# A four-byte store per partition behind the sin table, with a memset that waits for it, in an interleaved-RoPE kernel

## The chip, the core and the metric

The kernel runs on one core of one Trainium2 chip. The metric is the device time in microseconds (us); lower is better. The profile is taken from one execution; its span (315.8 us before) is a little shorter than the device time (317.56 us), and all times inside the profile count from the start of that span. DVE is the vector engine, ACT the scalar engine, POOL the GpSimd engine, SP the sync engine. A queue name such as ACTq is the sequencer of that engine, where DMAs are issued. A packet is one record of the trace for the DMA engines; a semaphore packet is the four-byte one that reports the end of a transfer on one engine, and a transfer has landed when all of them have arrived. The records don't name the engine: 16 packets of one kind at one time are read here as one on each of the 16.

## The reference

Rotary embedding on interleaved pairs. x has shape (8, 2048, 16, 64), float32; cos and sin have shape (2048, 32).

```python
out1 = x1 * cos - x2 * sin      # x1, x2: even and odd elements of the last axis
out2 = x1 * sin + x2 * cos
out  = np.stack([out1, out2], axis=-1).reshape(x.shape)
```

## The kernel before

Each of the 128 partitions holds 16 rows of each of the 8 batches. The GpSimd queue loads a batch and casts it from float32 to bfloat16 on the way (8.4 MB read, 4.2 MB written), DVE rotates it in place, and the GpSimd queue stores it and casts it back. There are five tiles, so five loads can be issued at once; loads 5, 6 and 7 each reuse a tile and wait for a store to land. The first two rows of batch 0 come through the SP and Activation queues, as do the tables.

```python
    def load(b, k0=0):
        if b not in tiles:
            tiles[b] = xpool.tile([P, K, HD], bf16, name="xt")
        nc.gpsimd.dma_start(out=tiles[b][:, k0:], in_=x_t[b, :, k0:])

    def store(b, k1=K):
        nc.gpsimd.dma_start(out=out_t[b, :, :k1], in_=tiles[b][:, :k1])
# ... rotate(): three tensor_tensor on DVE for four rows: q = x*s, x = x*c, x = x + swap(q) ...
    with tc.manual_schedule():
        # ... two head rows of batch 0, one on the SP and one on the Activation queue ...
        nc.sync.dma_start(out=cos_sb, in_=cos_t)
        nc.scalar.dma_start(out=sin_sb, in_=sin_t)
        load(0, HEAD)
        for b in range(1, NX):
            load(b)
        # ... ACT casts the head rows; DVE builds s_tab and c_tab from sin_sb and cos_sb ...
        for b in range(B):
            # ... rotate batch b, four rows at a time ...
            if b < B - 1:
                store(b)
            if b >= 1 and b - 1 + NX < B:
                load(b - 1 + NX)
        store(B - 1, K - TAIL)
        # ... the last four rows: cast on ACT once store 6 has landed, store on SP ...
```

## Time and profile before

| what | value | where it is read |
|---|---|---|
| time, median of 3 | 317.56 us | runs |
| DVE busy | 221.8 us, 70% of the span | busy table |
| GpSimd DMA queue | 97.0% of the time of 16 DMA engines | queue table |
| first rotation on DVE | 25.05 us | timeline |
| DVE's waits for loads | 5.92 + 10.76 us | timeline |

The first fence has, from the page of the kernel before, the busy share of DVE and of the DMA engines in 40 equal slices (tenths; 9 is 90% or more), and the queue table (packets, MB, share of the 16 engines' span).

```profile
DVE  0009999999999999999999994799708996000000
DMA  9999999999999999999999999999999999999997
...
q0 software_dynamic: 2304, 98.04, 97.0%
q1 hardware_dynamic: 432, 2.88, 2.4%
q10 hardware_dynamic: 288, 0.79, 0.6%
```

The DMA row has no gap; DVE has gaps at the start, twice in the second half and at the end. The DMA engines are the bound. Queue q0 is GpSimd's, q1 SP's, q10 Activation's.

The next fence is the timeline of POOL before: start, length, engine, line, operation, output and input, and in brackets how long POOL stood idle before and what ended that. L56 is a load, L59 a store.

```profile
1.25 2.79 POOL L56 DMA_DIRECT2D xt<-in_x_dram  x5 [0.80 <-PEq L145]
54.07 0.54 POOL L59 DMA_DIRECT2D out_dram<-xt  x1 [50.03 <-DVE xt L80]
81.72 0.54 POOL L59 DMA_DIRECT2D out_dram<-xt  x1 [27.11 <-DVE xt L80]
121.98 0.53 POOL L56 DMA_DIRECT2D xt<-in_x_dram  x1 [39.72 <-DMA out_dram<-xt]
122.50 0.53 POOL L59 DMA_DIRECT2D out_dram<-xt  x1
141.30 0.53 POOL L56 DMA_DIRECT2D xt<-in_x_dram  x1 [18.27 <-DMA out_dram<-xt]
...
193.40 0.53 POOL L59 DMA_DIRECT2D out_dram<-xt  x1 [12.39 <-DVE xt L80]
227.21 0.53 POOL L59 DMA_DIRECT2D out_dram<-xt  x1 [33.27 <-DVE xt L80]
258.87 0.53 POOL L59 DMA_DIRECT2D out_dram<-xt  x1 [31.13 <-DVE xt L80]
```

Issue and transfer are two things. Store 0 was issued at 54.07 us, when DVE had finished batch 0. But the queue runs its transfers one after the other, and five loads were ahead of it. The times at which the transfers of this queue ended, from the semaphore packets in the packet records of the trace, are: loads 0 to 4 at 23.7, 43.0, 62.4, 81.7 and 102.0 us; store 0 at 121.3; store 1 at 140.6; load 5 at 160.0; store 2 at 179.3; and so on, one every 19.3 us (load 4 took 20.3). So store 0 had 48 us to spare before its turn came, and store 1 had 40.

Two lines of the timeline of DVE before show where it waited for loads in the second half:

```profile
25.05 1.22 DVE L74 TENSOR_TENSOR qt<-xt,s_tab 128x2048 bf16<-128x2048 bf16 x1
...
199.03 2.29 DVE L74 TENSOR_TENSOR qt<-xt,s_tab 128x4096 bf16<-128x4096 bf16 x1 [5.92 <-DMA xt<-in_x_dram]
...
237.67 2.29 DVE L74 TENSOR_TENSOR qt<-xt,s_tab 128x4096 bf16<-128x4096 bf16 x1 [10.76 <-DMA xt<-in_x_dram]
```

### The profile page before, as it was taken

The page shows a single profiled execution, that of the slowest core. Times are in us where ns is not written, and L with a number is a line of the kernel's source. Part 1 is how long each engine was busy: PE and PEld are TensorE (multiplying, and loading weights), DVE is VectorE, ACT ScalarE, POOL GpSimd, SP SyncE. Part 2 cuts the span into 40 slices and gives each one's busy share as a digit, 9 for nine tenths or more (in the row PEclk, how much of TensorE's full clock was granted, in tenths as well). Part 3 has the DMA queues.
Part 4 walks back from the last instruction along what each step waited for, and adds up shares of the span by engine and source line. Part 5 has one row for each costly group of instructions (what it writes and reads, how often), then busy time and mean ns, then how long its engine had stood idle before and what let it go on. Part 6 is the DMA issues. An engine that isn't in the chain of part 4 may idle for free.

```text
span 315.8 us, 198 instructions
## 1 busy us (share of the span) xinstructions
DVE 221.8 (70%) x102; ACT 6.9 (2%) x4; POOL 8.8 (3%) x20
## 2 busy tenths in 40 slices
DVE  0009999999999999999999994799708996000000
ACT  2100000000000000000000000000000000000400
POOL 3000000000000001010000100000000000000000
DMA  9999999999999999999999999999999999999997
GB/s 267 211 248 203 199 208 257 199 199 245 220 199 266 398 465 465 398 332 246 220 398 398 390 208 199 448 481 266 199 266 465 398 398 506 423 398 440 427 427 299
DMA packets 3025, 101.72 MB, mean 322 GB/s; under 512 B 336, under 2 KB 336, under 8 KB 848
## 3 DMA queue, kind: packets, MB, share of 16 engines
q0 software_dynamic: 2304, 98.04, 97.0%
q1 hardware_dynamic: 432, 2.88, 2.4%
q10 hardware_dynamic: 288, 0.79, 0.6%
q14 instruction: 1, 0.01, 0.0%
HBM read 67.63 MB, written 67.11 MB: 427 GB/s over the span
## 4 chain that ended last, share of the span: by engine, by line
another core or an unknown queue 91%; DMA 2%; ACTq 1%; ACT 1%; issue 0%
DMA st<-in_x_dram 2%; ACTq L145 1%; ACT xt L93 1%; ACT L93 0%; ACT xt L117 0%; ACTq L117 0%; ACTq L93 0%
## 5 line engine op out<-in xcount | busy, mean ns | idle before, releaser
L74 DVE TENSOR_TENSOR qt<-xt,s_tab 128x4096 bf16<-128x4096 bf16 (+1 forms) x33 | 73.5, 2228 | 17.7 <-DMA xt<-in_x_dram 16.7
L80 DVE TENSOR_TENSOR xt<-xt,qt 128x4096 bf16<-128x4096 bf16 (+1 forms) x33 | 73.5, 2228 | 1.1
L75 DVE TENSOR_TENSOR xt<-xt,c_tab 128x4096 bf16<-128x4096 bf16 (+1 forms) x33 | 73.5, 2228 | 1.1
L95 DVE CAST s_tab<-sin_sb 128x512 bf16<-128x512 f32 x1 | 0.5, 454 | 23.8 <-DMA sin_sb<-in_sin_dram 23.8
L59 POOL DMA_DIRECT2D out_dram<-xt x8 | 4.3, 533 | 153.9 <-DVE xt L80 153.9
L56 POOL DMA_DIRECT2D xt<-in_x_dram x8 | 4.4, 560 | 96.4 <-DMA out_dram<-xt 95.6
L117 ACT COPY xt<-xt 1x1 bf16<-1x1 bf16 x1 | 0.2, 194 | 286.8 <-DMA out_dram<-xt 286.8
L118 ACT CAST st<-xt 128x4096 f32<-128x4096 bf16 x1 | 3.6, 3598 | 0.0
L93 ACT CAST xt<-st 128x2048 bf16<-128x2048 f32 x1 | 1.9, 1897 | 0.0
L93 ACT ACT_TABLE_LOAD x1 | 1.3, 1283 | 5.7 <-DMA st<-in_x_dram 5.7
L97 DVE CAST c_tab<-cos_sb 128x1024 bf16<-128x1024 f32 x1 | 0.7, 684 | 0.0
L96 DVE TENSOR_SCALAR s_tab<-sin_sb 128x512 bf16<-128x512 f32 x1 | 0.4, 444 | 0.0
L134 POOL MEMSET const-float32-0.0<- 128x1 f32 x1 | 0.1, 99 | 0.2 <-issue 0.2
L134 POOL MEMSET const-bfloat16-1.0<- 128x1 bf16 x1 | 0.1, 102 | 0.0
L134 POOL MEMSET const-float32-1.0<- 128x1 f32 x1 | 0.1, 99 | 0.0
L134 POOL MEMSET const-uint8-127<- 128x1 uint8 x1 | 0.1, 99 | 0.0
## 6 DMA issues: line engine op xcount, KB each, us to landing
xt<-in_x_dram POOLq DMA_DIRECT2D x7, 4096.0 KB, 57.6
out_dram<-xt POOLq DMA_DIRECT2D x1, 6144.0 KB, 53.0
xt<-in_x_dram POOLq DMA_DIRECT2D x1, 3584.0 KB, 22.8
out_dram<-st SPq DMA_DIRECT2D x1, 2048.0 KB, 15.5
st<-in_x_dram ACTq DMA_DIRECT2D x1, 512.0 KB, 5.1
st<-in_x_dram SPq DMA_DIRECT2D x1, 512.0 KB, 4.9
sin_sb<-in_sin_dram ACTq DMA_DIRECT2D x1, 256.0 KB, 22.6
cos_sb<-in_cos_dram SPq DMA_DIRECT2D x1, 256.0 KB, 18.6
```

What stands on the lines that cost most here:

```text
L56: nc.gpsimd.dma_start(out=tiles[b][:, k0:], in_=x_t[b, :, k0:])
L59: nc.gpsimd.dma_start(out=out_t[b, :, :k1], in_=tiles[b][:, :k1])
L74: nc.vector.tensor_tensor(out=rows(qt[:, :nk]), in0=rows(xp), in1=tab(s_tab), op=mult)
L75: nc.vector.tensor_tensor(out=rows(xp), in0=rows(xp), in1=tab(c_tab), op=mult)
L80: nc.vector.tensor_tensor(out=x3, in0=x3, in1=q_swap, op=add)
L93: nc.scalar.copy(out=tiles[0][:, :HEAD], in_=head[:, :HEAD])
L95: nc.vector.tensor_copy(out=s2[:, :, 0], in_=sin_sb)
L96: nc.vector.tensor_scalar_mul(s2[:, :, 1], sin_sb, -1.0)
L97: nc.vector.tensor_copy(out=c_tab.rearrange("p k (i j) -> p (k i) j", j=2), in_=cos_sb.to_broadcast([P, K * D2, 2]),)
L118: nc.scalar.copy(out=tail, in_=tiles[B - 1][:, K - TAIL :])
L134: nc = _bacc.Bacc("TRN2", target_bir_lowering=False, num_devices=1)
L145: with _tile.TileContext(nc) as tc:
```

## The change

A tile of one float32 per partition is set to zero and written to the first element of each partition's first output row, over the Activation queue, behind the sin table. The real result of store 0 overwrites it later. After the tables have been built, the word is set to zero again. That second memset overwrites the source of the small store, so it must wait until the store has landed; and as it stands before the rotations in DVE's program, every rotation waits behind it.

```diff
         nc.scalar.dma_start(out=sin_sb, in_=sin_t)
+
+        word = consts.tile([P, 1], fp32)
+        nc.vector.memset(word, 0.0)
+        nc.scalar.dma_start(out=out_t[0, :, 0, :1], in_=word)
         load(0, HEAD)
 ...
             in_=cos_sb.to_broadcast([P, K * D2, 2]),
         )
+
+        nc.vector.memset(word, 0.0)
         for b in range(B):
```

## The prediction

> **What bounds the kernel now.** The 16 DMA engines. The queue table gives the GpSimd queue 97.0% of the engines' span, and the DMA row is full in every slice. DVE is busy 221.8 of 315.8 us. The chain of waits names almost nothing (91% "unknown queue"), so I went by the DMA packet records: the GpSimd queue runs its 16 transfers one after the other, about 19.3 us each (8 packets of 2.45 us per engine, load or store): five loads until about 102 us, store 0 to 122, store 1 to 141, load 5 to 160, store 2 to 179, load 6, store 3, load 7, stores 4 to 7; the tail store ends the span. There is no hole.
>
> **What the change does.** By the instruction order: a memset before the sin cast and one after the table build on DVE, a 128x1 store on the Activation queue behind sin. The second memset overwrites the word, so it waits for that store to land, and all rotations stand behind it on DVE.
> When does it land? In the packet records sin's 2 KB packets (8 per engine, 0.09 us each) went one per turn, each followed by a 2.1 us packet of load 0; sin landed 22.6 us after issue, with load 0. The Trainium skill, "DMA: Bandwidth & Descriptors", section "Queues, rings and completion order", says engines go round-robin between rows by packet; the trace agrees. The word store is 8 four-byte packets plus a semaphore packet per engine on the same ring, so it needs 8 to 9 turns beside load 1: 19.3 to 21.8 us after 23.8. I expect it at 43 to 46 us, and the first rotation at 44 to 46 us instead of 25.05.
>
> **How much is critical.** The shift (about 20 us) goes into slack: stores issue when DVE is done, but their turn in the full queue comes later. Before, batch ready against start of transfer: store 0 54 / 102, store 1 82 / 122, store 2 109 / 160, store 3 137 / 199, store 4 165 / 238. Shifted by 20: 74, 102, 129, 157, 185, all in time; the tightest (store 1) keeps about 20 us. Later loads wait for landings that don't move. DVE's two waits for loads (5.9 and 10.8 us, timeline) shrink to nothing and absorb 16.7 us, so DVE ends some 3 to 6 us later, about 270 us; store 7's turn is at 295. The tail waits for store 6 (295.6), unchanged.
> On the critical resource there remain the word's packets, 9 per engine. Four-byte semaphore packets took 0.01 to 0.04 us here, so 0.1 to 0.4 us, an estimate. The same page (section "Specifications") says transfers under 512 B cause a read-modify-write; no run here shows yet what a four-byte HBM write takes.
>
> **Predicted time: 317.9 us, 8 in 10 between 317.2 and 319.0. Faster by over 2%: 1%; within 2%: 96%; slower: 3%.**
>
> **What would show each step.** Waits: the second memset waits about 20 us for the word's store. Timeline: first rotation about 45 us; stores 0 and 1 issued 20 us later; loads 5, 6, 7 issued at unchanged 122, 141, 180 us. DVE's wait for loads near 0. DMA row still full.
>
> **What would make it wrong.** If small packets go several per turn, the shift is 3 to 5 us (same time). If the shift passes 40 us, store 1 misses its turn and the engines idle. If a four-byte HBM write blocks an engine for 1 us, 9 add 9 us (3%). If DVE activity slows packets (no sign: 2.43 to 2.45 us with DVE idle or busy).

## The result, and the profile after

After: 317.64 us median (317.43 to 318.0, 6 runs); before, in the same rounds: 317.54 us (317.42 to 317.64, 6 runs). The ratio is 1.0005 with a 95% interval of 0.9992 to 1.0018: the same. All runs of before lie within 0.22 us of each other. A ratio is the mean time of one kernel's fast runs over that of the other's of the same rounds, so it is not quite the ratio of the medians quoted.

The same rows of the page after:

```profile
DVE  0001049999999999999999999999999998000000
DMA  9999999999999999999999999999999999999997
...
q0 software_dynamic: 2304, 98.04, 97.0%
q1 hardware_dynamic: 432, 2.88, 2.4%
q10 hardware_dynamic: 432, 0.79, 0.7%
```

The DMA row is as full as before. Queue q10 has 144 packets more: 16 engines with 8 data packets and one semaphore packet each. DVE starts two slices later, and its gaps in the second half are gone.

The start of DVE, from its timeline after:

```profile
24.72 0.68 DVE L101 CAST c_tab<-cos_sb 128x1024 bf16<-128x1024 f32 x1
43.44 0.06 DVE L106 MEMSET word<- 128x1 f32 x1 [18.03 <-DMA out_dram<-word]
43.51 1.23 DVE L74 TENSOR_TENSOR qt<-xt,s_tab 128x2048 bf16<-128x2048 bf16 x1
```

The memset, 0.06 us long, waited 18.03 us for a store of 512 bytes, and the first rotation starts at 43.51 instead of 25.05 us: a shift of 18.46 us. The timeline of POOL after, to be read against the one of before:

```profile
1.25 2.79 POOL L56 DMA_DIRECT2D xt<-in_x_dram  x5 [0.81 <-PEq L151]
72.52 0.54 POOL L59 DMA_DIRECT2D out_dram<-xt  x1 [68.48 <-DVE xt L80]
100.17 0.54 POOL L59 DMA_DIRECT2D out_dram<-xt  x1 [27.11 <-DVE xt L80]
121.92 0.53 POOL L56 DMA_DIRECT2D xt<-in_x_dram  x1 [21.22 <-DMA out_dram<-xt]
128.08 0.53 POOL L59 DMA_DIRECT2D out_dram<-xt  x1 [5.62 <-DVE xt L80]
141.39 0.53 POOL L56 DMA_DIRECT2D xt<-in_x_dram  x1 [12.79 <-DMA out_dram<-xt]
...
260.65 0.53 POOL L59 DMA_DIRECT2D out_dram<-xt  x1 [20.40 <-DVE xt L80]
```

Stores 0 and 1 are issued 18.45 us later, load 5 at 121.92 against 121.98 us, load 6 at 141.39 against 141.30 us, and the last store only 1.78 us later. Of the shift of 18.46 us, 5.92 + 10.76 = 16.68 us went where DVE had waited for loads 6 and 7 before, and 18.46 - 16.68 = 1.78 us is left at the end. The transfers of the GpSimd queue ended at the same times as before, within 0.1 us.

Why did 512 bytes take 41.6 us from issue to landing? The packet records of the changed kernel answer it. This table, in an ordinary fence, is worked out from them: packets of one kind that started within 1 us of each other are one group (count, first and last start in us).

```
load 1, 32 KB written:  16: 23.10-23.68   16: 25.52-26.09   16: 27.93-28.51  ...  16: 40.01-40.58
Activation queue, 4 B:  32: 23.07-23.67   16: 25.51-26.09   16: 27.93-28.50  ...  16: 40.00-40.58   8: 42.50-43.00
```

Until about 23.1 us the word's packets stood behind sin's on their own queue. From then on each engine takes one four-byte packet, then one packet of load 1, which takes it 2.4 us, then the next four-byte packet: one turn each. (The first group has two on each engine, because load 0's semaphore packet also went between 23.08 and 23.65 us; eight of its 32 are sin's semaphore packets. Half of the engines were one packet ahead of the rest; their last packet went with the group at 40.00, that of the others at 42.50 us.) The words themselves took 0.009 to 0.022 us each.

### The profile page after: what moved, and what is told of

The parts are those of the page before. It is cut to its first block, busy times and chain, and to the rows that moved or that the text cites. A ratio compares the mean times of both kernels' runs of the same rounds, so it can differ in the third digit from the quotient of the medians.

```text
span 315.8 us, 204 instructions
## 1 busy us (share of the span) xinstructions
DVE 222.0 (70%) x104; ACT 6.9 (2%) x4; POOL 8.9 (3%) x20
## 4 chain that ended last, share of the span: by engine, by line
another core or an unknown queue 91%; DMA 2%; ACTq 1%; ACT 1%; issue 0%
DMA st<-in_x_dram 2%; ACTq L151 1%; ACT xt L97 1%; ACT L97 0%; ACT xt L123 0%; ACTq L123 0%; ACTq L97 0%
```

## The experiments

My theory has three parts. First, the delay is a matter of turns: a small store waits once per packet behind one large packet. Second, the shift of DVE costs nothing while each store is issued before its turn in the full queue. Third, the engines' time is what counts, and the word's packets take almost none of it. The rivals: the store takes long in itself (a fixed time, or slow four-byte writes); the shift costs something that the change gives back elsewhere; the shift never matters at all. All ten kernels gave correct results. The diffs are against the changed kernel.

### e1_no_wait: the store without the wait

```diff
-        nc.vector.memset(word, 0.0)      # the second one
```

> The word's store stays, the second memset goes, so that nothing on DVE waits for it. My theory (turns in the ring, shift swallowed by slack, packets nearly free): first rotation back at about 25 us, the store still lands at about 43 us, time within 0.2% of before. Rival (the wait itself costs something that the packets or something else gives back in the changed kernel): time differs from before by over 0.3%.

Measured: 317.44 us (317.40 to 317.48, 5 runs) against 317.44 us of before; ratio 1.0000, 0.9986 to 1.0014. One line of its DVE timeline:

```profile
25.21 1.22 DVE L74 TENSOR_TENSOR qt<-xt,s_tab 128x2048 bf16<-128x2048 bf16 x1
```

The first rotation was back at 25.21 us, and the store still took 41.5 us to land. The packets alone cost nothing that can be seen.

### e2_delay_only: the wait without the store

```diff
-        nc.vector.memset(word, 0.0)
-        nc.scalar.dma_start(out=out_t[0, :, 0, :1], in_=word)
 ...
-        nc.vector.memset(word, 0.0)
+        nc.vector.tensor_copy(out=word, in_=tiles[1][:, 0, :1])
```

> No word store at all; DVE instead copies one word of load 1 after the tables are built, so it waits for the landing of load 1. My theory: the wait ends at about 43.2 to 43.5 us as with the word's store (within 1 us), first rotation at 43.5 to 44.5 us, same issue times of all stores as in the changed kernel, time within 0.2% of before. Rival (the delay of DVE costs or gains time of itself): a difference over 0.3%.

Measured: 317.51 us (317.49 to 317.70, 5 runs) against 317.44 us; ratio 1.0003, 0.9991 to 1.0016. One line of its DVE timeline:

```profile
43.45 0.15 DVE L104 CAST word<-xt 128x1 f32<-128x1 bf16 x1 [18.07 <-DMA xt<-in_x_dram]
```

A wait for load 1 ends at the same moment as the wait for the word (43.45 against 43.44 us), and the stores are issued at 72.55 and 100.19 us as in the changed kernel. Together with e1_no_wait: neither half of the change costs or gains time, so nothing was being cancelled. It also fits the turns, by which the word lands with load 1.

### e3_two_words, e4_three_words, e5_four_words: how much slack there is

```diff
-        nc.scalar.dma_start(out=out_t[0, :, 0, :1], in_=word)
+        for c in range(2):               # 3 and 4 in the others
+            nc.scalar.dma_start(out=out_t[0, :, 0, c : c + 1], in_=word)
```

> Two word stores, one behind the other, and the memset waits for both. My theory: the second lands one load later, at about 62.6 us; first rotation at about 63 us (shift 37.7); store 0 ready at 92 against its turn at 102, store 1 at about 119.5 against its turn at 121.5: still just in time, time within 0.5% of before. Rival (no such slack; each us of shift beyond the first few costs): some 10 to 20 us slower.

> Three word stores: landing at about 82 us, shift 57. My theory: stores 0 and 1 miss their turns. Store 0 is ready at 111 with the queue empty since 102 (hole of about 9 to 10 us), store 1 at 139 with the queue empty since 130 (hole of about 9 us); together about 19 us, time about 336.5 us (333 to 340). The DMA row shows two dips near 102 and 130 us. Rival (the shift never matters, as it is off the path): about 317.7.

> Four word stores that DVE waits for: landing at about 102 us, shift 76.5. My theory: past the slack the time grows with the shift one to one: about 19 us more than with three word stores, about 356 us (351 to 361); the holes are each about 28.5 us after 102 us and about 9 us before store 1. Rival (growth of another slope, as the loads that come later fill the holes): under 345.

| stores of a word | memset waited, us | store 0 issued | store 1 issued | time, us | ratio to before (95%) |
|---|---|---|---|---|---|
| 1 (the change) | 18.0 | 72.52 | 100.17 | 317.64 | 1.0005 (0.9992 to 1.0018) |
| 2 | 37.5 | 92.06 | 119.70 | 317.71 | 1.0008 (0.9995 to 1.0022) |
| 3 | 56.7 | 111.26 | 138.91 | 336.77 | 1.0608 (1.0594 to 1.0623) |
| 4 | 76.1 | 130.41 | 158.05 | 356.58 | 1.1228 (1.1212 to 1.1243) |

Each further store adds 19.2 to 19.5 us of wait, the length of one load. With two, the timeline of POOL has stores 0 and 1 so:

```profile
92.06 0.54 POOL L59 DMA_DIRECT2D out_dram<-xt  x1 [88.02 <-DVE xt L80]
119.70 0.54 POOL L59 DMA_DIRECT2D out_dram<-xt  x1 [27.10 <-DVE xt L80]
```

Store 1 was issued 1.4 us before store 0's transfer ended (121.1 us), and the time did not move. This was the very edge: store 1's first packets started at 120.80 us, 1.1 us after the issue, and by then most of the engines had ended store 0 (they ended it between 120.2 and 121.1 us), so that they stood empty for 0.25 us on average. The slack thus ends about 1.1 us before the turn itself. With three, both stores came too late. The stages in which that shows, by windows of the profile (window, length, busy time of DVE, ACT and POOL with counts, clock, share of the DMA engines, GB/s), first with three words:

```profile
95.00:101.00 6.00, 5.93 (x3) 0.00 (x0) 0.00 (x0) 1.00 0.81 175
101.00:114.00 13.00, 12.80 (x7) 0.00 (x0) 0.54 (x1) 1.00 0.19 81
114.00:130.00 16.00, 15.76 (x8) 0.00 (x0) 0.00 (x0) 1.00 1.07 459
130.00:142.00 12.00, 11.83 (x6) 0.00 (x0) 1.07 (x2) 1.00 0.21 87
142.00:160.00 18.00, 17.73 (x9) 0.00 (x0) 0.00 (x0) 1.00 1.09 437
```

and the same windows of the changed kernel with its one word:

```profile
95.00:101.00 6.00, 5.90 (x4) 0.00 (x0) 0.54 (x1) 1.00 0.96 175
101.00:114.00 13.00, 12.80 (x7) 0.00 (x0) 0.00 (x0) 1.00 1.12 479
114.00:130.00 16.00, 15.80 (x7) 0.00 (x0) 1.06 (x2) 1.00 0.93 397
130.00:142.00 12.00, 11.79 (x7) 0.00 (x0) 0.53 (x1) 1.00 1.03 394
142.00:160.00 18.00, 17.76 (x8) 0.00 (x0) 0.53 (x1) 1.00 1.08 262
```

(A packet is counted in the window in which it starts, so shares can pass 1.) With three words the DMA engines are mostly empty around 101 to 114 and 130 to 142 us, before store 0 and before store 1; DVE is as busy in both kernels. By the packet records load 4 ended at 101.1, store 0 at 131.8 and store 1 at 159.5 us; less 19.3 us each for the transfers, the holes, in which the queue had nothing to move, are 11.4 and 8.4 us. From there on a transfer ended every 19 to 20 us again. With four words load 4 ended at 101.2, store 0 at 151.0 and store 1 at 178.6 us: holes of 30.5 and 8.3 us. The time rose by 19.3 us from before to three words (336.77 - 317.44) and by 39.0 us to four (356.58 - 317.60, of the other rounds), 19.7 us more for 19.15 us more of shift. With three words store 1 was issued 138.91 - 121.3 = 17.6 us after its turn had come in the kernel before, and its transfer ended 20.6 us after its issue in place of 19.3, as its first packets started only at 140.0 us, 1.1 us after the issue: together 18.9 of the 19.3 us that were lost. Both rivals, a cost per us of shift and no cost at all, are ruled out: the cost is zero up to the slack, and about one to one beyond, by the two kernels past it.

### e6_sixteen, e7_sixtyfour: packets per engine

```diff
-        nc.scalar.dma_start(out=out_t[0, :, 0, :1], in_=word)
+        nc.scalar.dma_start(out=out_t[0, :16, 0, :1], in_=word[:16])   # :64 in the other
```

> The word is written on 16 partitions alone: one data packet and one semaphore packet per engine in place of eight and one. My theory (one packet per turn): it lands about 2.4 us after sin, at about 26 us; first rotation at 26 to 27 us. Rival (a store of this kind takes a fixed time under load, or waits for load 1 as a whole): still about 43 us. Time as before, within 0.3%.

> The word is written on 64 partitions: four data packets and one semaphore packet per engine. My theory: four turns of 2.42 us after sin, landing at about 33 to 34 us, first rotation right behind. Rival: about 43 us, as with 128. Time as before, within 0.3%.

One line each from the waits of the two kernels (16 partitions first; engine, line and what it waited for, us in total, times, longest):

```profile
DVE word L106 <- DMA out_dram<-word: 1.2, 1, 1.2
```

```profile
DVE word L106 <- DMA out_dram<-word: 8.4, 1, 8.4
```

With 1, 4 and 8 data packets per engine the second memset ran at 26.41, 33.65 and 43.44 us: (33.65 - 26.41) / 3 = 2.41 us and (43.44 - 33.65) / 4 = 2.45 us per packet, one large packet each. A fixed time of the store is ruled out. The times, one run each with the state unknown, were 317.79 and 317.61 us against 317.65 us of before.

### e8_word_first: the same store before the large loads

```diff
+        word = consts.tile([P, 1], fp32)
+        nc.vector.memset(word, 0.0)
+        nc.scalar.dma_start(out=out_t[0, :, 0, :1], in_=word)
         head = stage.tile([P, TAIL, HD], fp32, name="st")
 ...      # and these three lines go from behind sin
```

> The same 128-partition word store, now first on the Activation queue, before any load of the GpSimd queue has packets in the engines. My theory: with no large packets to take turns with, it lands within 2 to 4 us of its issue; the second memset waits for nothing, first rotation at about 25 to 27 us. Rival (each four-byte write to HBM takes about 2.4 us of itself): it lands about 20 us after issue and drags the head and sin behind it to about 20 to 45 us. Time as before, within 0.3%.

The issues of its Activation queue, by the DMA view (output and input, queue, operation and count, KB, us from issue to landing):

```profile
st<-in_x_dram ACTq DMA_DIRECT2D x1, 512.0 KB, 11.7
sin_sb<-in_sin_dram ACTq DMA_DIRECT2D x1, 256.0 KB, 29.8
out_dram<-word ACTq DMA_DIRECT2D x1, 0.5 KB, 4.1
```

The word landed 4.1 us after its issue, a tenth of the 41.6 us in the changed kernel, with the same eight packets per engine. So four-byte writes to HBM are not slow in themselves. One number of my expectation missed: the first rotation came at 32.91 us, not at 25 to 27. By the packet records the head row's first packet on this queue started at 4.32 us, behind the word, instead of at 2.55 us in the kernel before, and the large packets of load 0 began at 5.4 us, before the head row was through; the rest of the head row and then sin took turns with them (head 11.7 us instead of 5.1, sin 29.8 instead of 22.6). That is the same mechanism at another place, but I had left it out. The time was 317.47 us against 317.65 us (one run, state unknown).

### e9_wide: 4096 bytes per partition

```diff
-        word = consts.tile([P, 1], fp32)
+        word = consts.tile([P, HD], fp32)
 ...
-        nc.scalar.dma_start(out=out_t[0, :, 0, :1], in_=word)
+        nc.scalar.dma_start(out=out_t[0, :, 0], in_=word)
```

> The store is 4096 bytes per partition in place of 4: still eight data packets per engine, so the same turns. My theory: lands at about 43 to 45 us, DVE shifted as in the changed kernel (within 2 us), but each engine has 8 packets of about 0.16 us more, so the time rises by about 1.2 us (0.4%), to 318.4 to 319.3, since only engine time counts. Rival (small writes cost more than their bytes by a read-modify-write): no rise, or a fall, against the changed kernel.

Measured: 318.70 us (318.62 to 319.07, 5 runs) against 317.65 us; ratio 1.0038, 1.0024 to 1.0051. The memset ran at 44.85 us. The Activation queue's packets took each engine 3.41 us in sum instead of 2.19, which is 1.22 us more, and the ratio stands for 1.2 us. The transfers of the GpSimd queue ended 1.0 to 1.4 us later than before from load 1 on, and store 1, issued at 102.29 us, was far from its turn, so the rise is not the shift of DVE. A thousand times the bytes changed the landing by 1.4 us, and engine time went into the result about one to one.

### e10_many: eleven stores that nothing on DVE waits for

```diff
         nc.scalar.copy(out=tiles[0][:, :HEAD], in_=head[:, :HEAD])
+        word = consts.tile([P, 1], fp32)
+        nc.vector.memset(word, 0.0)
+        for c in range(11):
+            nc.scalar.dma_start(out=out_t[B - 1, :, K - 1, c : c + 1], in_=word)
 ...      # the store behind sin and the second memset are taken out
```

> Eleven word stores, to addresses that the tail store alone overwrites, issued behind the head cast; DVE does not wait for them. 99 small packets per engine in place of 9. My theory: they land one per transfer of the GpSimd queue, the last at about 236 us; the engines lose 99 times about 0.02 us, so the time rises by about 1 to 3 us (0.3 to 1%); per store of one word that is 0.1 to 0.3 us. Rival (a four-byte write is free): no rise over 0.2%. Rival (it blocks the engine for about 1 us): 80 us or more.

Measured: 318.19 us (318.07 to 318.53, 5 runs) against 317.60 us; ratio 1.0021, 1.0007 to 1.0035. The last of the eleven landed at about 238 us, as turns would have it. The rise is there, but smaller than I had said: 0.6 us for 99 packets per engine, about 6 ns each (2 to 11 ns by the interval). One store of nine packets would by that cost some 0.05 us, an estimate that no run of one store can show. The summed packet times would have misled here; the queue table of this kernel says:

```profile
q0 software_dynamic: 2304, 98.04, 96.8%
q10 hardware_dynamic: 1872, 0.79, 22.8%
q1 hardware_dynamic: 432, 2.88, 2.4%
```

The shares sum to 122%. Beside loads a four-byte packet is on record with 0.02 us or less, but beside stores five of every nine are with 2.4 or 4.9 us, one or two lengths of a large packet. If it held the engine for that time, 22.8% of the span would be some 70 us; the time rose by 0.6. Such a record contains waiting beside the large packets. What it waits for there the records don't show, and I leave it open.

## Why the prediction was right

- The bound: right. The DMA row is full in both kernels, the transfers of the GpSimd queue ended at the same times within 0.1 us, and e9_wide shows that added engine time appears in the result.
- The landing of the word, 43 to 46 us by eight to nine turns: 43.3 us (the memset ran at 43.44), at the lower end, as half of the engines finished with the eighth turn and the others one turn later, beside load 1's own semaphore packet. The turns are shown by the packet records and by e6_sixteen and e7_sixtyfour; e8_word_first rules out a slow write.
- The shift, "about 20 us": 18.46 us; the first rotation, at 43.51 us, came a little before the 44 to 46 us that I gave. DVE's waits for loads vanished as said, and DVE ended 1.8 us later, not 3 to 6, only because the shift was smaller than I had rounded it to.
- The slack of "about 20 us" at store 1: with the change store 1 was issued at 100.17 us and its turn came at 121.3, 21 us later. A second word used up 19.5 us of that without a cost that can be seen, and left none; a third cost 19.3 us.
- The cost of the packets, 0.1 to 0.4 us: too high. By e10_many it is about 0.05 us. The term was too small for this to matter to the forecast of 317.9 us; the median was 317.64, within the stated 317.2 to 319.0.

## What to carry to other kernels

Where a queue is full, compare when a transfer is issued with when its turn comes: the difference, less the time from issue to first packet (1.1 us here), is how much its producer may slip for free, and beyond it each microsecond of slip cost about a microsecond here. The landing of a small DMA beside a queue of large ones was here a matter of its packets per engine times the length of one large packet, not of its bytes, so put it ahead of the large transfers or on fewer partitions if something waits for it. Look also at what stands behind it on its own queue, as e8_word_first showed.

## What the Trainium skill lacked or had wrong

- "DMA: Bandwidth & Descriptors", section "Anatomy of one DMA — SWDGE (gpsimd) path", gives about 2.0 us plus bytes over 436 GB/s per DMA, fitted for that path; the page has no such estimate for a small DMA of the scalar queue beside a busy GpSimd queue. Here 512 bytes took 41.6 us behind sin and 4.1 us ahead of the loads, and each packet per engine added 2.4 us.
- The same page, section "Queues, rings and completion order", says that an engine drains a packet of typically 9 to 17 descriptors before it switches rows. The round-robin is borne out, but here a turn of the Activation queue was one partition's row (2048 or 4 bytes), and one of the GpSimd queue one row of 64 KB on the float32 side (2.43 us for a load); the records don't show how many descriptors such a row is.
- The same page, section "Specifications", says that transfers under 512 bytes cause a read-modify-write. What that costs is not said; 99 four-byte writes and semaphores per engine cost 0.6 us of the total here, about 6 ns each.
- "Trainium Kernel Development and Optimization", section "Key Constraints", says that DMAs of the three queues interleave on the same 16 engines. It does not say that packet durations can then overlap: in e10_many the queues' shares sum to 122%, and 4-byte packets are on record with up to 4.9 us.
